# Loading weights for a split-fp32 decoder kernel: from a fixed lead of four half products to a lead set by free buffers

## The chip, the cores and the metric

The kernel runs on one core of a Trainium2 chip. It has a matrix engine (PE, with its weight loads shown apart as PEld), a vector engine (DVE), a scalar engine (ACT), GpSimd (POOL), and SyncE (SP), which here only issues DMAs. The metric is the device time of one execution in microseconds (us). Where time is broken down, it is one execution recorded by the hardware profiler.

## The reference

Two decoder layers on 512 tokens of width 2048, in fp32. Each layer projects its input to three groups of heads, attends, gates, projects back and normalizes (cut to what is computed):

```python
def hybrid_layer(x, mem, w_in, b_forget, w_mem_kv, w_out, ln_gain, ln_bias):
    h = jnp.einsum('bsd,dn->bsn', x, w_in)
    (fq, fk, fv, fg, f_logit, dq, dk, dv, dg,
     iq, ik, iw, mq, mg) = jnp.split(h, offsets, axis=-1)
    log_f = jax.nn.log_sigmoid(f_logit + b_forget)
    y_fox = fox_attention(fq, fk, fv, jnp.cumsum(log_f, axis=1)) * jax.nn.silu(fg)
    y_dsa = dsa_attention(rope(dq), rope(dk), dv, rope(iq), rope(ik), iw * 16 ** -0.5) * jax.nn.silu(dg)
    k_mem, v_mem = jnp.split(jnp.einsum('bmd,dn->bmn', mem, w_mem_kv), 2, axis=-1)
    y_mem = memory_attention(mq, k_mem, v_mem) * jax.nn.silu(mg)
    y = jnp.einsum('bsn,nd->bsd', jnp.concatenate([y_fox, y_dsa, y_mem], -1), w_out)
    return layer_norm(ALPHA * x + y, ln_gain, ln_bias)

def reference(x, mem, w_in, ...):
    for l in range(2):
        x = hybrid_layer(x, mem, w_in[l], ...)
    return x
```

The fox heads have a causal bias from the cumulated forget gates, the dsa heads choose 128 keys per query by an index score, and the memory heads attend to 256 fixed tokens.

## The kernel before

**Products of split numbers.** Each fp32 operand is split in a high and a low part, and a product is high x high, high x low and low x high. The weights come in 274 chunks of 128 x 2048 (1 MB), each used as two half products of 128 x 1024 (512 KB), so there are 548; half product n is half n % 2 of chunk n // 2. Most take 12 matmuls, those of the indexer 24. The value, gate and output projections run as seven products on 2 x 2 blocks in place of eight, so their operands are sums of blocks.

**Where a half product's weights come from.** Four ways, listed per chunk by `stream()`: 146 chunks are read from the weights as they are ("wall"); 44 from a sum that POOL's DMAs had added up in DRAM earlier ("sum", L553 to L571); 20 are loaded raw, with two further tiles ("other", L379) that DVE adds (`pair_w`, "pair"); and 64 are a raw buffer that is kept and has another block added to it ("grown", in `grow_w` by a DMA that accumulates, in `make_w` by DVE), which needs no load.

**The way of a load.** `load_w` takes one of seven raw buffers and issues the load on SP (L373). ACT copies it to a high part (`whi`), DVE subtracts that from the raw data to get the low part (`wlo`); both go to a pool of four pairs (`split_w`, helper at L242). A buffer is free once its low part is written, or, where it is to grow, once the grown product is split. In the main loop (L1602), half product n first has the loads for chunk i + 2 issued, that is for half product n + 4; for a "pair" and for the first chunks, both halves go out at the first one (L1640 to L1645). Then come the split of n + 3, the additions for a pair of n + 4, the matmuls of n, and a choice of other work.

**What sets the order.** A planner with a clock for PE, ACT, DVE and POOL (class `Clock`, L197) fits the other work between the products; it charges nothing for SP. SP works through a single list in the order in which the program was written out, and an entry whose target is not free, or whose source is not yet written, holds all behind it. Besides the raw loads, this list has the transposed reads of stored values (`load_turned`, L1378), the decay rows of the fox heads (ck, L935), head tiles (L1349, L1389), stored partial sums (L1323), and, for the normalization that runs on into layer 1, the gain and bias rows (L1455) and the residual tiles z (L1519).

**Stages.** Layer 0: values and gates from about 160 to 530 us, heads (the last value products with attention between them) to 810, output projection to 930. Layer 1: memory, indexer and small projections to 1060, values to 1471, heads to 1751, output to 1884.

Of the kernel before, what the change touches and what calls it, by code (L numbers as in the profile page):

```python
# [35 lines left out]
SCALE = HD ** -0.5  # L36
SOON, LATER, URGENT, DUE = 1.5, 4.0, 5.0, 10.0
SLOTS = 69
PACE = 2
R_ATTEND, R_QK, R_LOAD, R_MEM = 4, 5, 4, 8  # L40

# [216 lines left out]
def kernel(  # L258
# [13 lines left out]
    clock = Clock()  # L272
    nc = Engines(tc.nc, clock)
    consts = ctx.enter_context(tc.tile_pool(name="consts", bufs=1))
    raws = ctx.enter_context(tc.tile_pool(name="raws", bufs=7))
    whl = ctx.enter_context(tc.tile_pool(name="whl", bufs=4))
    slots = ctx.enter_context(tc.tile_pool(name="slots", bufs=SLOTS))
    tiny = ctx.enter_context(tc.tile_pool(name="tiny", bufs=3))
# [52 lines left out]
    chunks = stream()  # L331
    raw, parts = {}, {}
# [22 lines left out]
    def load_w(i, pieces=2, some=(0, 1)):  # L355
        if i < len(chunks) and chunks[i][4][0] != "grown":
            kind, key = chunks[i][4]
            src = {"wall": lambda: wall[key], "sum": lambda: sums[key],
                   "pair": lambda: wall[key[0]]}[kind]()
            if chunks[i][0] == "out" and chunks[i][2][0] == "P7":  # L360
                for h in some:
                    t = [slot("grown") for _ in range(2)]
                    raw.setdefault(i, []).append(t)
                    for c in range(2):
                        nc.sync.dma_start(t[c], half(src, h)[:, c * 512:(c + 1) * 512])
                return
            w = DM // pieces
            for c in range(pieces):
                if c * 2 // pieces not in some:
                    continue  # L370
                if c * 2 % pieces == 0:
                    raw.setdefault(i, []).append(raws.tile([P, H], F32, tag="raw", name=uid("raw")))
                nc.sync.dma_start(raw[i][-1][:, c * w % H:c * w % H + w], src[:, c * w:(c + 1) * w])  # L373
                if i < 3 and c * 2 % pieces == 0:
                    load_mem(2 * i + c * 2 // pieces)
                if kind == "pair":
                    for e in (2 * c, 2 * c + 1):
                        t = others[i, e] = slot("other")
                        nc.sync.dma_start(t, wall[key[1]][:, e * 512:(e + 1) * 512])  # L379

    others = {}

    def pair_w(n):

        i, h = divmod(n, 2)
        if i < len(chunks) and chunks[i][4][0] == "pair":
            for e in range(2):
                d = raw[i][h][:, e * 512:(e + 1) * 512]
                nc.vector.tensor_tensor(d, d, others.pop((i, 2 * h + e)), op=ALU.add)
# [163 lines left out]
    def add_weights(key, src):  # L553
        nc.gpsimd.dma_start(sums[key], src, accum_op=ALU.add, max_dma_last_dim=2 * DM)

    def weight_sums(kind, l, names, pairs, some=(0, 1)):

        for name in names:
            for n in some:
                step = SUM_STEPS[name][n]  # L560
                for pair in pairs:
                    for g in range(2):
                        key = (kind, l, name, pair, g)
                        src = block(kind, l, pair, g, step)
                        pool_waits()
                        if n:
                            add_weights(key, src)
                        else:
                            sums[key] = dram.tile([P, DM], F32, name=uid("sum"))
                            nc.gpsimd.dma_start(sums[key], src, max_dma_last_dim=2 * DM)  # L570
                        yield  # L571
# [1030 lines left out]
    for i, (kind, l, j, col, _) in enumerate(chunks):  # L1602
        late = last_half(i)
        if kind == "out":
            step = OUT_ORDER.index(j)
            name, pair = j
# [28 lines left out]
        for h in range(2):  # L1635
            n = 2 * i + h
            grow_w(n + 2)
            if n in late_makes:
                make_w(late_makes[n])
            if i > 0:  # L1640
                late_half = i > 8 and i + 2 < len(chunks) and chunks[i + 2][4][0] != "pair"
                if late_half:
                    load_w(i + 2, 2, (h,))
                elif h == 0:
                    load_w(i + 2)  # L1645
            if h == 0 and i > 0:
                if 2 <= i < 6:
                    for k in range(4 * i - 8, 4 * i - 4):
                        load_xt(k)
                elif i == 7:  # L1650
                    load_tables()
            if n < 6:
                split_mem(n + 2)
            if n in splits:
                finish_flow(splits.pop(n))
            if ahead_of(i):
                splits[n + 3] = flow(split_steps(n + 3), 1e9, clock.at["PE"] + DUE)
            else:
                split_w(n + 3)
            pair_w(n + 4)  # L1660
            for k in range(2 * n - 20, 2 * n - 18) if n < 16 else range(12, 16) if n == 16 else ():
                if k >= 0:
                    split_x(k)
            if kind == "out" and late:

                for e, w in enumerate(parts[n]):
                    kept.append((left[aname, 2 * col + h], e, w))
                    rows_product(zs[0], 0, kept[-1:], len(kept) == 1, h == col == e == 1, not opens)
                if h == col == 1:
                    residual(0, (2, 3)[name == "Q3"], zs[0], last=True)  # L1670
                if len(kept) == 16:
                    finish_at_once(0)
                    rows_product(chains["b", 1][1], 1, kept[:8], True, True)
                    residual(1, 2, chains["b", 1][1], last=True)
                    for c in (0, 256):
                        ps = bank("z")
                        c = slice(c, c + 256)
                        rows_product(ps, 1, kept[8:], True, True, c=c)
                        residual(1, 3, ps[:, c], 1, c, True)
                    finish_at_once(1)  # L1680
            elif kind == "out":
                for st in range(2):
                    for e in range(2):
                        r = slice(e * 256 + st * P, e * 256 + (st + 1) * P)
                        product(zs[st], tuple(a[:, r] for a in left[aname, 2 * col + h]),
                                tuple(a[:, e * 512:(e + 1) * 512] for a in parts[n]),
                                opens and col == h == e == 0,
                                col == h == e == 1, not opens)
                        advance()
            elif kind == "vs":  # L1690
                for st in range(2):
                    for e in range(2):
                        product(zs[st], val_left(aname, 2 * col + h, e, st),
                                tuple(a[:, e * 512:(e + 1) * 512] for a in parts[n]),
                                opens and col == h == e == 0, col == h == e == 1, not opens)
                        advance()
                    if col == h == 1:
                        val_out(name, pair, st, zs[st])
            elif kind == "mv":
                for m in range(2):  # L1700
                    for nn in range(2):
                        k = 4 * col + 2 * h + nn
                        c = (k % 2) * 256 + m * P
                        product(out_ps[m], tuple(a[:, c:c + P] for a in memT[k // 2]),
                                tuple(a[:, nn * 512:(nn + 1) * 512] for a in parts[n]),
                                k == 0, k == KT - 1)
            elif kind == "mk":
                for kk in range(8):
                    k = 8 * h + kk
                    m = memT[k // 2]  # L1710
                    c = (k % 2) * 256
                    product(ps[:, :256], weight_cols(n, kk), tuple(a[:, c:c + 256] for a in m),
                            k == 0, k == KT - 1)
            else:
                cols = slice(P if kind == "iq" else 0, SEQ)
                for kk in range(8):
                    k = 8 * h + kk
                    product(ps[:, cols], weight_cols(n, kk), tuple(a[:, cols] for a in xT[k]),
                            k == 0, k == KT - 1)
                    advance()  # L1720
            del parts[n]
            if h == 0:
                tick(kind, kind in ("out", "vs"))
# [174 lines left out]
```

## Time and profile before

| what | value |
|---|---|
| median of 3 runs | 1885.79 us (1884.57 to 1889.16) |
| the profiled execution: own time, span | 1885.75 us, 1884.0 us |
| mean granted clock of PE | 0.997 |
| ACT, whi from raw | 497 times, 1056 ns each |
| DVE, wlo from raw and whi | 497 times, 1217 ns each |
| PE, one matmul of the value products, 128 x 512 | about 227 ns from start to start |
| raw loads on SP, 512 KB each | 331 from the weights, 72 from sums |
| issue to landing of a raw load, median | 7.3 and 7.4 us |
| loads of "other", 256 KB each | 80, 13.7 us to landing |
| data moved | 478.40 MB, mean 254 GB/s |

A matmul's start-to-start time comes from 12 matmuls in 2.72 us. A row of a wait names who waits (engine, tile, line), then behind the arrow whose work ended the wait, and the total, the number and the longest. In a timeline, the numbers in brackets are the idle time ahead of an instruction and what ended it. "SPq" is SyncE's DMA issue. Names such as raw, whi, wlo, z, ck are the program's tile names. Nearly all compute instructions carry the line of one helper, L242, so they are told apart by their tiles.

### The profile page before, as it was taken

The numbers are of one execution on the slowest core, as the hardware profiler recorded it, in microseconds if no ns is written. First come the engines' busy times: TensorE is split into PE (matmuls) and PEld (weight loads), VectorE is DVE, ScalarE is ACT, GpSimd is POOL, SyncE is SP. The second block draws the span as 40 slices with busy tenths as digits, with TensorE's granted clock in tenths as the row PEclk, the third lists the DMA queues.
The fourth block names the chain that finished last, engine by engine and source line by source line (L and its number), as shares of the span: only waits on it lengthen the run. The fifth ranks groups of instructions, "written<-read, shape, count | busy, mean of one in ns | idle before, by whom it ended". The sixth has DMA issues, their size and how long they took to land.

```text
span 1884.0 us, 26451 instructions
## 1 busy us (share of the span) xinstructions
PE 1854.5 (98%) x8994; PEld 1574.5 (84%) x8994; DVE 1606.9 (85%) x2565; ACT 1079.0 (57%) x1752; POOL 404.9 (21%) x595
## 2 busy tenths in 40 slices
PE   9999999999999999999999999999999999999997
PEld 8998888887888888888899977877878888888886
DVE  6789889888789987889887997898797898878798
ACT  5776344435347887555476653444354578875553
POOL 0121222122134311330011121221221343113302
PEclk9999999999999999999999999999999999999999
DMA  9885998898999978986598869988989998889866
GB/s 350 294 240 160 302 298 242 303 279 274 253 239 298 241 217 218 268 209 214 174 322 250 228 204 302 329 270 288 284 274 246 247 306 226 222 213 276 237 215 144
DMA packets 232165, 478.40 MB, mean 254 GB/s; under 512 B 76624, under 2 KB 101200, under 8 KB 231772
## 3 DMA queue, kind: packets, MB, share of 16 engines
q1 hardware_dynamic: 177660, 302.58, 49.8%
q0 software_dynamic: 53792, 173.06, 35.7%
q8 instruction: 71, 1.16, 0.2%
q10 hardware_dynamic: 576, 1.05, 0.1%
q14 instruction: 66, 0.54, 0.1%
HBM read 404.24 MB, written 152.07 MB: 295 GB/s over the span
## 4 chain that ended last, share of the span: by engine, by line
PE 70%; DVE 14%; DMA 8%; issue 4%; ACT 3%; SPq 0%; POOL 0%; DVEq 0%; ACTq 0%; POOLq 0%
PE v L242 30%; PE c L242 17%; PE z L242 15%; DVE wlo L242 6%; DMA other<-in_wall_dram 4%; DMA raw<-in_wall_dram 3%; PE po L242 3%; DVE raw L242 2%; PE s L242 2%; DVE acc L242 1%; ACT whi L242 1%; PE ix L242 1%; PE pt L242 1%; DMA v<-vraw 1%; DVE rope L242 1%
## 5 line engine op out<-in xcount | busy, mean ns | idle before, releaser
L242 ACT ACTIVATE whi<-raw 128x1024 fp32r<-128x1024 f32 (+1 forms) x497 | 521.2, 1056 | 473.5 <-PE v L242 190.9
L242 DVE TENSOR_TENSOR wlo<-raw,whi 128x1024 fp32r<-128x1024 f32 (+1 forms) x497 | 601.0, 1217 | 115.8 <-ACT whi L242 113.6
L242 PE MATMUL v<-whi,vxh 128*128 128x512 f32 x768 | 306.3, 399 | 6.8 <-ACT whi L242 3.2
L242 PE MATMUL v<-wlo,vxh 128*128 128x512 f32 x768 | 301.4, 392 | 7.9 <-DVE wlo L242 7.9
L242 PE MATMUL v<-whi,vxl 128*128 128x512 f32 x768 | 300.5, 391 | 0.0
L242 PE MATMUL v<-whi,xh 128*128 128x512 f32 x576 | 224.2, 389 | 0.0
L242 PE MATMUL v<-whi,xl 128*128 128x512 f32 x576 | 224.1, 389 | 0.0
L242 PE MATMUL v<-wlo,xh 128*128 128x512 f32 x576 | 224.1, 389 | 0.0
L242 PE MATMUL c<-xh,whi 128*128 128x512 f32 (+1 forms) x544 | 197.9, 364 | 0.0
L242 PE MATMUL c<-xh,wlo 128*128 128x512 f32 (+1 forms) x544 | 197.8, 364 | 0.0
L242 PE MATMUL c<-xl,whi 128*128 128x512 f32 (+1 forms) x544 | 197.7, 363 | 0.0
L242 POOL TENSOR_TENSOR seen<-mark,mhalf 128x1 f32<-128x1 f32 x88 | 48.3, 549 | 636.3 <-ACT mark L242 447.3
L242 PEld LDWEIGHTS v<-whi,vxh 128*128 128x128 f32 x768 | 144.7, 188 | 40.1 <-ACT whi L242 7.2
L242 PEld LDWEIGHTS v<-wlo,vxh 128*128 128x128 f32 x768 | 144.9, 189 | 39.3 <-DVE wlo L242 12.5
L242 PE MATMUL z<-wlo,yh 128*128 128x512 f32 (+1 forms) x434 | 167.8, 387 | 2.3 <-DVE wlo L242 2.3
L242 PEld LDWEIGHTS v<-whi,vxl 128*128 128x128 f32 x768 | 144.5, 188 | 30.4
L242 PE MATMUL z<-whi,yh 128*128 128x512 f32 (+1 forms) x434 | 168.6, 389 | 0.0
L242 PE MATMUL z<-whi,yl 128*128 128x512 f32 (+1 forms) x434 | 167.7, 387 | 0.0
L242 PEld LDWEIGHTS v<-wlo,xh 128*128 128x128 f32 x576 | 108.1, 188 | 22.6
L242 PEld LDWEIGHTS v<-whi,xh 128*128 128x128 f32 x576 | 108.1, 188 | 22.5
L242 PEld LDWEIGHTS v<-whi,xl 128*128 128x128 f32 x576 | 108.1, 188 | 22.5
L242 PEld LDWEIGHTS c<-xl,whi 128*128 128x128 f32 x544 | 102.1, 188 | 12.2
(209 smaller groups left out, 3459.9 us busy)
## 6 DMA issues: line engine op xcount, KB each, us to landing
raw<-in_wall_dram SPq DMA_DIRECT2D x331, 512.0 KB, 7.3
sum<-in_wall_dram POOLq DMA_DIRECT2D x88, 1024.0 KB, 10.4
raw<-sum SPq DMA_DIRECT2D x72, 512.0 KB, 7.4
v<-vraw POOLq DMA_DIRECT2D x88, 256.0 KB, 8.8
other<-in_wall_dram SPq DMA_DIRECT2D x80, 256.0 KB, 13.7
vt<-halves POOLq DMA_DIRECT2D x56, 256.0 KB, 9.4
vraw<-v SPq DMA_DIRECT2D x56, 256.0 KB, 5.1
grown<-in_wall_dram POOLq DMA_DIRECT2D x48, 256.0 KB, 8.9
```

The source lines that it names most:

```text
L242: return f(*args, **kw)
```

## The change

A half product's load is issued by a new function `load_half`, which remembers in `loaded` what is out. The load for n + 4 stays. After it, when chunk 8 is past, `load_more` looks ahead from n + 4 and issues up to two further half products, up to n + 14, skipping those that grow. It stops where fewer than two of the seven raw buffers would be left by the program's count (`raws_used() >= RAWS - 1`), at one product of the output projection, at a pair while more than two of the "other" tiles are outstanding, and at a sum whose last addition the planner issued less than 20 us ago by its own clock (`settled`). A pair's two halves now also go out one by one.

```diff
+RAWS, FAR, SETTLE = 7, 14, 20.0
...
-    raws = ctx.enter_context(tc.tile_pool(name="raws", bufs=7))
+    raws = ctx.enter_context(tc.tile_pool(name="raws", bufs=RAWS))
...
+    loaded, settled = set(range(6)), {}
+
+    def load_half(m):
+        if m not in loaded:
+            loaded.add(m)
+            load_w(m // 2, 2, (m % 2,))
+
+    def raws_used():
+        return len({id(t) for v in raw.values() for t in v if t is not None and not isinstance(t, list)})
+
+    def load_more(n):
+
+        m = n + 4
+        for _ in range(2):
+            while m in loaded or (m < 2 * len(chunks) and chunks[m // 2][4][0] == "grown"):
+                m += 1
+            if m > n + FAR or m >= 2 * len(chunks) or raws_used() >= RAWS - 1:
+                return
+            kind, l, j, _, (how, key) = chunks[m // 2]
+            if kind == "out" and j[0] == "P7" or how == "pair" and len(others) > 2:
+                return
+            if how == "sum" and settled.get(key, 1e9) + SETTLE > clock.at["PE"]:
+                return
+            load_half(m)
...
                             add_weights(key, src)
+                            settled[key] = clock.at["PE"]
...
             if i > 0:
-                late_half = i > 8 and i + 2 < len(chunks) and chunks[i + 2][4][0] != "pair"
-                if late_half:
-                    load_w(i + 2, 2, (h,))
-                elif h == 0:
-                    load_w(i + 2)
+                for m in (n + 4,) if i > 8 else (n + 4, n + 5) if h == 0 else ():
+                    load_half(m)
...
             pair_w(n + 4)
+            if i > 8:
+                load_more(n)
```

Lines below move by one (L373 is L374) and further down by 27 (L1378 is L1405, L935 is L962, L1455 is L1482, L1519 is L1546). The instructions of PE, ACT, DVE and POOL stand in the same order as before; the list of SP has the same 753 rows in another order. Three places of it follow. A row has the line, the operation, the target and its source, and the shape; numbers at the names count tiles in the order of writing.

SP where layer 0's heads begin (raw: weights, from the weights or a sum; vraw: values of a head read transposed; ck: decay rows), before:

```order
L373 DMA raw_5107<-sum_1132 128x1024
L1378 DMA_TRANSPOSE vraw_5116<-vt_168 128x1x1024
L1378 DMA_TRANSPOSE vraw_5118<-vt_170 128x1x1024
L935 DMA ck_5120<-crow_159 128x512
L1378 DMA_TRANSPOSE vraw_5122<-vt_168 128x1x1024
L1378 DMA_TRANSPOSE vraw_5124<-vt_170 128x1x1024
L935 DMA ck_5126<-crow_159 128x512
L373 DMA raw_5157<-sum_1132 128x1024
L373 DMA raw_5244<-sum_1264 128x1024
L373 DMA raw_5281<-sum_1264 128x1024
```

and with the change:

```order
L374 DMA raw_5002<-sum_1142 128x1024
L374 DMA raw_5028<-sum_1142 128x1024
L374 DMA raw_5052<-sum_1274 128x1024
L374 DMA raw_5074<-sum_1274 128x1024
L374 DMA raw_5096<-in_wall_dram 128x1024
L374 DMA raw_5121<-in_wall_dram 128x1024
L1405 DMA_TRANSPOSE vraw_5126<-vt_168 128x1x1024
L1405 DMA_TRANSPOSE vraw_5128<-vt_170 128x1x1024
L962 DMA ck_5130<-crow_159 128x512
L1405 DMA_TRANSPOSE vraw_5132<-vt_168 128x1x1024
L1405 DMA_TRANSPOSE vraw_5134<-vt_170 128x1x1024
L962 DMA ck_5136<-crow_159 128x512
```

The second half of the first sum, both halves of the next sum and two loads of plain weights now stand ahead of the four transposes and of both decay rows: five loads that stood behind them.

SP in layer 1 ahead of the first value products (row: gain and bias of layer 0's normalization; z: a tile of its residual), before:

```order
L1519 DMA z_10760<-x_183 128x512
L373 DMA raw_10786<-in_wall_dram 128x1024
L373 DMA raw_10851<-sum_9319 128x1024
L373 DMA raw_10910<-sum_9319 128x1024
L1455 DMA row_10952<-in_gain_dram 128x512
L1455 DMA row_10954<-in_bias_dram 128x512
L1519 DMA z_10956<-x_183 128x512
L373 DMA raw_10978<-in_wall_dram 128x1024
L373 DMA raw_11003<-in_wall_dram 128x1024
L373 DMA raw_11046<-sum_10096 128x1024
L373 DMA raw_11068<-sum_10096 128x1024
```

and with the change:

```order
L1546 DMA z_10522<-x_183 128x512
L374 DMA raw_10553<-sum_9329 128x1024
L374 DMA raw_10611<-sum_9329 128x1024
L374 DMA raw_10678<-in_wall_dram 128x1024
L374 DMA raw_10742<-in_wall_dram 128x1024
L1546 DMA z_10770<-x_183 128x512
L374 DMA raw_10921<-sum_10106 128x1024
L1482 DMA row_10958<-in_gain_dram 128x512
L1482 DMA row_10960<-in_bias_dram 128x512
L1546 DMA z_10962<-x_183 128x512
L374 DMA raw_10989<-sum_10106 128x1024
```

Of the four raw loads that stood behind the rows, the two of plain weights and the first half of the sum now stand ahead of them; the sum's second half stays behind.

SP in layer 1's values, the stretch that was issued around 1180 to 1199 us, before:

```order
L1455 DMA row_11985<-in_gain_dram 128x512
L1455 DMA row_11987<-in_bias_dram 128x512
L1519 DMA z_11989<-x_183 128x512
L373 DMA raw_11994<-in_wall_dram 128x1024
L373 DMA raw_12014<-in_wall_dram 128x1024
L373 DMA raw_12042<-in_wall_dram 128x1024
L373 DMA raw_12060<-in_wall_dram 128x1024
L373 DMA raw_12084<-in_wall_dram 128x1024
L379 DMA other_12086<-in_wall_dram 128x512
L379 DMA other_12088<-in_wall_dram 128x512
```

and with the change:

```order
L1546 DMA z_11853<-x_183 128x512
L374 DMA raw_11879<-in_wall_dram 128x1024
L374 DMA raw_11902<-in_wall_dram 128x1024
L374 DMA raw_11920<-in_wall_dram 128x1024
L374 DMA raw_11953<-in_wall_dram 128x1024
L374 DMA raw_11975<-in_wall_dram 128x1024
L380 DMA other_11977<-in_wall_dram 128x512
L380 DMA other_11979<-in_wall_dram 128x512
L1482 DMA row_11999<-in_gain_dram 128x512
L1482 DMA row_12001<-in_bias_dram 128x512
L1546 DMA z_12003<-x_183 128x512
```

The rows and the z tile, which stood ahead of five raw loads and the other tiles of a pair, now stand behind them.

## The prediction

> **What bounds the kernel now.** I read the page first (the span, part 1), then the busy times by stretch, then the waits of the stretches where the matrix engine sits idle. Each stretch row has its length, the busy time of PE, PEld, DVE, ACT and POOL with counts, the granted clock, the DMA share and GB/s.
>
> ```profile
> span 1884.0 us, 26451 instructions
> PE 1854.5 (98%) x8994; PEld 1574.5 (84%) x8994; DVE 1606.9 (85%) x2565; ACT 1079.0 (57%) x1752; POOL 404.9 (21%) x595
> ...
> 530.00:810.00 280.00, 278.03 (x1415) 235.04 (x1414) 240.03 (x442) 204.01 (x397) 73.44 (x98) 1.00 0.91 251
> 1060.00:1090.00 30.00, 30.00 (x154) 26.96 (x153) 27.60 (x44) 19.47 (x36) 4.26 (x7) 1.00 0.90 261
> 1090.00:1115.00 25.00, 22.65 (x102) 18.21 (x101) 24.12 (x36) 13.67 (x24) 6.02 (x9) 1.00 0.56 178
> 1165.00:1190.00 25.00, 23.47 (x95) 19.03 (x96) 23.91 (x33) 13.21 (x18) 5.81 (x10) 0.93 0.88 220
> 1190.00:1236.00 46.00, 44.59 (x196) 36.30 (x194) 36.23 (x55) 18.60 (x22) 10.86 (x16) 1.00 1.02 341
> 1236.00:1380.00 144.00, 140.21 (x611) 114.31 (x612) 125.68 (x172) 65.69 (x84) 28.52 (x49) 1.00 0.86 270
> 1751.00:1884.00 133.00, 120.23 (x553) 99.70 (x551) 116.55 (x195) 58.34 (x87) 31.88 (x42) 0.97 0.71 189
> ```
>
> PE is busy 1854.5 of 1884.0 us, so nothing that only shortens its waits can bring more than 29.5 us, and 12.77 of those (133.00 less 120.23) are the tail of the output product and of the normalization, of which the new loads touch nothing. The change only moves weight loads on SP. It can pay where a load is late for its split (ACT writes whi from raw, DVE then wlo from both), and that split is late for PE. The waits of 1060 to 1240 (total, times, longest):
>
> ```profile
> ACT whi L242 <- DMA raw<-in_wall_dram: 10.9, 8, 3.4
> DVE raw L242 <- DMA other<-in_wall_dram: 9.8, 7, 2.2
> ...
> PE v L242 <- DVE wlo L242: 3.9, 4, 1.8
> PE v L242 <- ACT whi L242: 1.6, 2, 0.8
> ```
>
> Of 10.9 + 9.8 us that ACT and DVE wait for weights here, PE feels 3.9 + 1.6 = 5.5 us. This is where loads bind. In the heads of layer 0 (530 to 810; layer 1's heads are the same code) PE's idle time is 280.00 - 278.03 = 1.97 us, and its releasers are results that go out of PSUM, no splits:
>
> ```profile
> PE v L242 <- ACT vraw L242: 0.8, 2, 0.5
> PE v L242 <- DVE vraw L242: 0.6, 1, 0.6
> PE v L242 <- DVE rec L242: 0.5, 1, 0.5
> ```
>
> **The change part by part.** The profiled execution took 1885.75 us (span 1884.0 and 1.75 around it); the sum is made against that. The median of the runs shown, 1885.79, is 0.04 us away. The orders of PE, ACT, DVE and POOL are unaltered, and SP issues the same DMAs, so no instruction is added or removed on any engine: only times of landing move. SP stands here with its idle time and work:
>
> ```profile
> 1047.46 1.07 SPq L373 DMA_DIRECT2D raw<-in_wall_dram  x1
> 1048.63 0.85 SPq L373 DMA_DIRECT2D raw<-sum  x2
> 1065.61 0.33 SPq L1455 DMA_DIRECT2D row<-in_gain_dram  x1
> ...
> 1067.53 1.24 SPq L373 DMA_DIRECT2D raw<-in_wall_dram  x2
> 1068.86 5.17 SPq L373 DMA_DIRECT2D raw<-sum  x2
> ...
> SPq L1455 <- DVE rope L242: 16.1, 1, 16.1
> SPq L1519 <- DMA x<-z: 7.3, 1, 7.3
> ```
>
> Term a, start of layer 1's values. SP stood 16.1 us at the load of a gain row, whose slot the rotary work freed late. Four weight loads stood behind it and went out at 1067.5 to about 1074. In the second order shown with the change, three of the four stand ahead of that row; they need only buffers, which splits free, and go out 11 to 19 us earlier. Their lateness shows as ACT's idle time in brackets, then in DVE, then in PE:
>
> ```profile
> 1080.88 1.06 ACT L242 ACTIVATE whi<-raw 128x1024 fp32r<-128x1024 f32 x1 [3.36 <-DMA raw<-in_wall_dram]
> 1084.72 2.24 ACT L242 ACTIVATE whi<-raw 128x1024 fp32r<-128x1024 f32 x2 [1.55 <-DMA raw<-in_wall_dram]
> ...
> 1085.82 1.23 DVE L242 TENSOR_TENSOR wlo<-raw,whi 128x1024 fp32r<-128x1024 f32 x1 [0.48 <-ACT whi L242]
> ...
> 1108.43 0.50 PE L242 MATMUL v<-wlo,vxh 128*128 128x512 f32 x1 [0.59 <-DVE wlo L242]
> 1113.21 0.50 PE L242 MATMUL v<-wlo,vxh 128*128 128x512 f32 x1 [1.76 <-DVE wlo L242]
> ```
>
> ACT's 3.36 + 1.55 us go, but DVE, which PE waits for, is busy 24.12 of 25 us, and only 0.48 us of its idle time came from a late whi. DVE cannot catch up more than that, in the order that it keeps. I take 0.5 us; the bounds are 0 and PE's whole idle time, 2.35 us (25.00 - 22.65).
>
> Term b, 1165 to 1190: PE is idle 25.00 - 23.47 = 1.53 us, and 1.35 more are lost to the clock (term c). In the third order shown, five raw loads and the two further blocks of a pair now stand ahead of two rows and a residual load that waited. The splits that PE waits for here stand behind pairs' additions; the 9.8 us of DVE's waits for "other" tiles are the row. The first of these pairs was issued before the place where the order differs, so only part can shift: I take 0.5, bounds 0 and 1.53.
>
> Term c, the clock. After two short waits the granted clock fell in 3 us to 0.55, which costs 3.00 x (1 - 0.55) = 1.35 us:
>
> ```profile
> 1167.00:1170.00 3.00, 2.96 (x8) 2.32 (x9) 2.95 (x5) 3.00 (x6) 1.99 (x3) 0.55 0.21 70
> ...
> 1165.78 0.50 PE L242 MATMUL v<-whi,vxh 128*128 128x512 f32 x1 [0.78 <-ACT whi L242]
> 1167.04 0.59 PE L242 MATMUL v<-wlo,vxh 128*128 128x512 f32 x1 [0.76 <-DVE wlo L242]
> ...
> 1234.88 0.50 PE L242 MATMUL v<-whi,vxh 128*128 128x512 f32 x1 [0.80 <-ACT whi L242]
> 1236.14 0.50 PE L242 MATMUL v<-wlo,vxh 128*128 128x512 f32 x1 [0.76 <-DVE wlo L242]
> ```
>
> A like pair of waits at 1234.88 and 1236.14 was followed by no loss (clock 1.00 in 1236 to 1380). So the loss hangs on the moment as well as on the waits. It may go, stay, or come at the other pair too (-1.35): I take half, 0.7 us. The Trainium skill, "TensorE: Matmul & The Clock Gate", section "HAM oscillation — how this bites in real kernels", has the clock fall when the engine idles for longer than about 3.4 us; by that rule neither pair of waits could have cost a clock, term c would be 0, and the sum 1884.1. This trace differs: 0.78 and 0.76 us of idle time stand right before the fall.
>
> Term d, 1190 to 1236: PE is idle 46.00 - 44.59 = 1.41 us. Four raw loads go out 2.4 us and more earlier, one split's pace each. But the transfers run at a share of 1.02 with 341 GB/s here, against 0.56 at 178 GB/s in 1090 to 1115: what is issued early shares its engines with what was issued before. I take half, 0.7 us; bounds 0 and 1.41. The Trainium skill, "DMA: Bandwidth & Descriptors", section "Issuing engines are not separate DMA queues", says that transfers interleave on the same 16 DMA engines whoever issued them; taken strictly, a stretch at a share of 1.02 gains nothing from issuing early, d is 0 and the sum 1884.1. The row of 1.02 speaks for it, that of 0.56 leaves room one stretch earlier.
>
> Term e, the heads: 0, since no split is among PE's releasers there. The cover is loads that land before their splits, and it is not gone as raws go out earlier still. What becomes late instead is the subject of the slower rival. Term f, 1236 to 1380: PE is idle 3.79 us, but from about 1240 on the two orders agree again: 0.
>
> Sum: 0.5 + 0.5 + 0.7 + 0.7 = 2.4 us; 1885.75 - 2.4 = 1883.4.
>
> **The rivals.** First: **nothing moves**. Seven buffers hold the data of 4 loads ahead, 2 being split and little else; the new rule reaches two further at most. Where the buffers bind, a load that stands earlier in the order starts when it did before, and ACT's 10.9 us of waits for raws mostly stay. For it: PE feels only 5.5 us; DVE, at 24.12 of 25, cannot use earlier data. Against it: SP's 16.1 us at a row load, with three free weight loads behind it. Time: 1885.75, with the loads' terms all 0. Chance 0.24.
>
> Second: **all waits for weights vanish**. From 1060 to 1236, PE's idle time is 2.35 + 1.53 + 1.41, and the clock's 1.35 goes with it: 6.6 us, so 1879.1; with half of the 3.79 us after it, 1877.2. For it: each wait in that region ends at a split or at what feeds one. Against it: DVE's 0.48, and pairs' other tiles, which come no earlier than the raws that they follow. Chance 0.22.
>
> Third, on the other side: **small loads queue behind weights** where the heads begin. One queue issues in order. In the first order shown, five further raw loads stand ahead of the turned values and of the decay rows (ck). Buffers come free at the splits' pace there:
>
> ```profile
> L242 ACT ACTIVATE whi<-raw x6: 1047/1059/1064, 531.0 to 542.9; 128x1024 fp32r<-128x1024 f32 x6
> ...
> 531.97 5.84 SPq L1378 DMA_TRANSPOSE vraw<-vt  x2
> ...
> DMA to landing us min/median/max: 4.5/5.5/8.4
> ...
> 543.31 0.37 POOL L242 TENSOR_SCALAR bt<-ck,cq 128x128 f32<-128x128 f32 x1 [8.39 <-DMA ck<-crow]
> 549.08 1.14 ACT L242 ACTIVATE qh<-vraw 128x512 fp32r<-128x512 f32 x2
> ...
> 553.55 1.06 ACT L242 ACTIVATE whi<-raw 128x1024 fp32r<-128x1024 f32 x1 [3.34 <-issue]
> ...
> 563.93 0.69 DVE L242 CUSTOM_DVE_ANT_0 bt<-s,bt 128x512 f32<-128x512 f32 x1 [0.51 <-PE s L242]
> ```
>
> Six splits in 531.0 to 542.9 are 2.4 us apart, (542.9 - 531.0) / 5, so five loads hold the first transpose from 531.97 to at most 531.97 + 11.9 = 543.9. With 4.5 to 8.4 us to land, its data comes at 548.4 to 552.3, and ACT reads them at 549.08: late by 3.2 at most, and a second group behind it alike, some 2.6. Two groups, 5.8 us, in two layers are 11.6: 1897.4 where all of it reaches PE, 1891.6 where half does. It decides from the point at which a transpose is issued after 549.08 - 5.5 = 543.6, or where the decay rows, waited for until 543.31, come more than some 10 us late, since their tables feed DVE at 563.93. Against it: the 3.34 us for which ACT is idle before 553.55 swallow the first lateness, and a buffer or two may be free earlier than 2.4 us per load. Chance 0.16, and my reason for the upper end.
>
> **How the numbers follow.** The forecast has 0.38, the rivals 0.24, 0.22 and 0.16. A measurement of this kernel can tell 0.3% from no change, 5.7 us: faster is below 1880.1, slower above 1891.4. The forecast and the first rival lie within; the second lies beyond only with nearly all its waits gone (most of its 0.22), and the third mostly beyond, with what other small load might come late. This gives 0.22 faster, 0.63 the same, 0.15 slower. The likeliest case alone, with its bounds (2.35 + 1.53 + 1.35 + 1.41 gained, or 1.35 lost to the clock), spans 1879.1 to 1887.1. The range for 8 in 10 goes from the second rival's 1877.2 to the third's half price: 1877 to 1892; left out are the third's full price and combinations.
>
> **What would show it.** Term a: SP's wait of 16.1 us may stay, but three weight loads stand ahead of it, ACT's waits for raws fall from 10.9 to under 6, and PE's 2.35 us in 1090 to 1115 fall by little. Terms b and d: PE's idle time in the two later stretches shrinks by a third to a half. Term c: a clock of 1.00 where 0.55 stood. Term e: PE's idle time in the heads stays near 2 us. The third rival would show as ACT's qh in the heads waiting for the DMA into vraw, POOL's 8.39 us for ck growing toward 20, and PE idle in 545 to 610. The forecast is wrong if DVE makes use of earlier data beyond 0.48 us, or if a transfer that nobody was late for before (rows, residuals, turned values) becomes late for an engine that works in order.

## The result and the profile after

The change made the kernel slower: 1900.7 us median of 6 runs against 1886.16 for the kernel before, ratio 1.0069 with a 95% interval of 1.0052 to 1.0086. The forecast was 1883.4 us in a range of 1877 to 1892; it was wrong. One of the six runs took 6083.61 us; the ratio goes by the other five, and nothing on record shows what held that run up. A later set of runs of the same kernel (f1 below) gave 1.0051 (1.0035 to 1.0068).

The head of the changed kernel's page:

```profile
span 1899.7 us, 26470 instructions
PE 1862.2 (98%) x8994; PEld 1579.9 (83%) x8994; DVE 1607.9 (85%) x2565; ACT 1082.4 (57%) x1752; POOL 398.7 (21%) x595
```

PE is busy 7.7 us longer for the same matmuls, and idle for the other half of the 15.7 us. Its busy times by stretch (length, busy PE, PEld, DVE, ACT, POOL, granted clock, DMA share, GB/s; the work of a stretch lies up to 13 us later than before, so a row does not hold quite the same work):

```profile
530.00:810.00 280.00, 274.17 (x1383) 231.32 (x1382) 236.79 (x439) 199.69 (x386) 71.04 (x102) 0.99 0.91 244
1090.00:1115.00 25.00, 25.00 (x116) 20.90 (x115) 24.63 (x38) 14.73 (x25) 2.25 (x4) 1.00 0.56 153
1165.00:1190.00 25.00, 24.16 (x106) 19.43 (x105) 21.49 (x29) 11.23 (x15) 3.69 (x6) 1.00 0.81 214
1190.00:1236.00 46.00, 44.47 (x188) 36.08 (x187) 36.40 (x58) 18.47 (x22) 11.67 (x19) 0.96 1.03 350
1236.00:1380.00 144.00, 140.58 (x604) 114.68 (x603) 121.25 (x165) 60.87 (x75) 28.45 (x45) 0.98 0.87 268
```

The stretch of the heads, where PE had lost 1.97 us, now loses 280.00 - 274.17 = 5.83, and its clock is 0.99. In the two stretches at 1090 and 1165 the idle time went from 2.35 to 0 and from 1.53 to 0.84 (in part because the waits moved out of them: PE is 8 us late by then), and the clock of 0.93 is 1.00.

Since PE's order is unaltered in every kernel here, each matmul can be paired with the same one of before, and the lag of its start read off. This table has by how much the lag grew in each stretch (times of the trace of before), in us: for the change, for its second execution f1, and as the mean, with the lowest and highest, over all traces of this study with further loads in that stretch and over those without (the experiments follow below):

| stretch | change | f1 | with further loads there | without |
|---|---|---|---|---|
| 428 to 445, layer 0's values | +3.0 | 0.0 | +3.0 (0.0 to 5.1), 6 traces | +1.1 (-0.2 to 3.9), 7 |
| 535 to 815, layer 0's heads | +5.5 | +4.7 | +5.5 (4.7 to 6.1), 4 | +0.3 (-0.4 to 0.9), 6 |
| 1100 to 1166, layer 1's values | -1.3 | -1.4 | -1.4 (-1.8 to -1.1), 7 | 0.0 (-0.9 to 1.1), 6 |
| 1166 to 1175 | -1.6 | -1.6 | -1.6 | -1.6 (all 13 within 0.1) |
| 1219 to 1250, rows and residual tiles | +7.6 | +4.5 | +5.7 (4.5 to 7.6), 4 | +1.1 (0.0 to 2.8), 9 |
| 1250 to 1465 | -1.7 | +0.4 | -1.6 (-3.1 to 0.4), after such a loss, 4 | 0.0 (-2.9 to 4.5), 9 |
| 1465 to 1745, layer 1's heads | +5.3 | +3.3 | +4.3 (3.3 to 5.3), 4 | +0.8 (0.2 to 1.5), 6 |
| the rest | -1.0 | -0.1 | | |
| sum | +15.8 | +9.8 | | |

In the rows of the heads, e1, e6 and e7 are left out, which have a part of the further loads there. The row at 1166 is alike in all: the profiled execution of before had a fall of the clock there that no other has, so its 1.6 us are luck and no gain of the change.

In the heads the waits name the mechanism. SP's timeline of the changed kernel, where before the first two transposes had gone out at 531.97:

```profile
534.46 6.57 SPq L374 DMA_DIRECT2D raw<-sum  x4
543.43 2.30 SPq L374 DMA_DIRECT2D raw<-in_wall_dram  x2
545.78 4.87 SPq L1405 DMA_TRANSPOSE vraw<-vt  x2
550.75 0.53 SPq L962 DMA_DIRECT2D ck<-crow  x1
```

Of the view of the tile vraw, 545 to 562 us, the row on its transfers:

```profile
DMA to landing us min/median/max: 4.1/5.6/6.0
```

The transposes go out 13.8 us later, 10.9 of them beyond the lag of 2.9 that PE had by then. They land as fast as before (median 5.6 us against 5.5): the lateness is all from standing behind raw loads on SP. Who waited is in the timelines of POOL, ACT, DVE and PE from there on and, last, of PE in layer 1's heads (idle time ahead and its releaser in brackets):

```profile
554.70 0.37 POOL L243 TENSOR_SCALAR bt<-ck,cq 128x128 f32<-128x128 f32 x1 [16.92 <-DMA ck<-crow]
...
555.51 0.63 ACT L243 ACTIVATE qh<-vraw 128x512 fp32r<-128x512 f32 x1 [2.95 <-DMA vraw<-vt]
...
578.75 0.63 ACT L243 ACTIVATE tanh<-vraw 128x512 f32<-128x512 f32 x1 [1.03 <-DMA vraw<-vt]
580.38 0.63 ACT L243 ACTIVATE vh<-vraw 128x512 fp32r<-128x512 f32 x1 [0.99 <-DMA vraw<-v]
...
585.95 0.50 PE L243 MATMUL v<-whi,vxh 128*128 128x512 f32 x1 [1.68 <-ACT vraw L243]
...
610.78 0.63 ACT L243 ACTIVATE qh<-vraw 128x512 fp32r<-128x512 f32 x1 [2.48 <-DMA vraw<-vt]
...
614.80 0.63 ACT L243 ACTIVATE vh<-vraw 128x512 fp32r<-128x512 f32 x1 [1.39 <-DMA vraw<-v]
...
617.34 1.23 DVE L243 TENSOR_TENSOR wlo<-raw,whi 128x1024 fp32r<-128x1024 f32 x1 [2.61 <-ACT whi L243]
...
619.83 0.50 PE L243 MATMUL v<-whi,vxh 128*128 128x512 f32 x1 [2.61 <-DVE vraw L243]
...
1568.59 0.50 PE L243 MATMUL v<-whi,vxh 128*128 128x512 f32 x1 [3.21 <-DVE vraw L243]
```

ACT's waits of 540 to 625 us (total, times, longest):

```profile
ACT qh L243 <- DMA vraw<-vt: 5.4, 2, 3.0
ACT vh L243 <- DMA vraw<-v: 2.4, 2, 1.4
ACT tanh L243 <- DMA vraw<-vt: 1.3, 2, 1.0
```

Before, ACT waits for none of these tiles in that stretch. Now ACT, which works in order, waits for a turned tile or a head tile six times, its weight splits and evictions slip behind, DVE waits for a split (at 617.34), and PE stands. After 619.83 the clock falls too: the lag grows by another 1.5 us with PE busy.

### The profile page after: what moved, and what is told of

It is laid out like the page before. It is cut to its first block, busy times and chain, and to the rows that moved or that the text cites. A ratio compares the mean times of both kernels' runs of the same rounds, so it can differ in the third digit from the quotient of the medians.

```text
span 1899.7 us, 26470 instructions
## 1 busy us (share of the span) xinstructions
PE 1862.2 (98%) x8994; PEld 1579.9 (83%) x8994; DVE 1607.9 (85%) x2565; ACT 1082.4 (57%) x1752; POOL 398.7 (21%) x595
## 5 line engine op out<-in xcount | busy, mean ns | idle before, releaser
L243 PE MATMUL v<-whi,vxh 128*128 128x512 f32 x768 | 309.0, 402 | 15.8 <-DVE vraw L243 5.8
```

Of the source, the lines that this page charges most:

```text
L243: return f(*args, **kw)
```

## The experiments

"Theory Q" is that of the third rival: small loads which other engines need in order stand behind raw loads on SP. "Theory C" is contention: more 512 KB transfers in flight make everything land later, anywhere. Each run is told as a ratio to runs of the kernel before on the same chip. In all of them the orders of PE, ACT, DVE and POOL are those of before.

**e1: the change without the heads' products.**

```diff
+            if kind == "vs" and j[0] in ("Q5", "Q3"):
+                return
```

> The full change, but no further load is issued when its target is one of the heads' products (Q5, Q3); the order of SP in the heads is as before the change. Theory Q (small loads that other engines need in order stand behind raw loads on SP): of the 15.7 us that the trace of the change lost, matmul by matmul 5.9 came in layer 0's heads and 4.9 in layer 1's, so this run should be 10.8 us faster than the change, about 1889 to 1891, and PE's idle time in the heads back near 2 us each. Theory C (the loss is contention and lost clock spread over the kernel): the run stays near 1897 to 1900.

1.0030 (1.0016 to 1.0044), 1893.91 us, against 1.0069 and 1.0051 for the whole change. The heads' waits for transposes are gone, but the run did not get down to 1889. PE's waits show a new one:

```profile
PE gt L243 <- DMA vraw<-v: 4.8, 2, 2.5
```

At the end of each layer's heads, three further raw loads for the output projection now stand ahead of two head tiles which PE itself turns: theory Q at a place that I had not listed. The expectation missed by this. The wait is e1's own: at these two matmuls PE waits 2.26 and 2.50 us in e1, and not at all in either trace of the whole change.

**e2: further loads around the heads alone.** The rule by which a pair's halves go out is that of before here, and in e3, e6, e7, f2, f3 and f4.

```diff
-            if i > 8:
+            if 157 <= n <= 217 or 431 <= n <= 491:
                 load_more(n)
```

> Further loads only while the products just ahead of the heads and those of the heads run (both layers), all else as before the change. Theory Q: plus 10.8 us over before, about 1896 to 1897, with ACT waiting some 3 us for a transposed value tile at the heads' start and POOL's wait for the decay rows near 17 us instead of 8.4. Theory C: a part in proportion to the further loads here, some 57 of about 230 per layer pair, so plus 3 to 5 us, and no wait for transposes.

1.0050 (1.0032 to 1.0068), 9.4 us by the ratio. The heads alone give most of what the change lost, and the waits are those that theory Q expected; theory C expected none for transposes:

```profile
ACT qh L243 <- DMA vraw<-vt: 4.6, 2, 2.8
ACT vh L243 <- DMA vraw<-v: 3.8, 2, 3.0
...
POOL bt L243 <- DMA ck<-crow: 31.9, 3, 16.8
```

**e3 and f4: only the start of layer 1.** The same kernel on two chips.

```diff
-            if i > 8:
+            if 283 <= n <= 340:
                 load_more(n)
```

> Further loads only from layer 1's first products to its 11th or so half product after the indexer, half products 283 to 340; later stretches, the heads and layer 0 as before. Theory Q: here loads overtake rows that nobody is late for, so PE gains what the change gained between 1100 and 1170 us, 3.1 us (0.8 of a wait, 0.75 of another, 1.5 of the clock): about 1883. Theory C: no gain, 1886 or above.

> The same kernel as e3, once more on another chip. Theory Q: the gain of e3 repeats, 0.997 to 0.999. If e3 was luck of its runs, 1.000.

0.9983 (0.9969 to 0.9998), then 0.9993 (0.9980 to 1.0006). From 1100 to 1166 us both profiled executions win at the expected place, 1.8 and 1.5 us, where the six traces without these loads have 0.0 on the mean. The 1.5 us of clock in the expectation were none of the change's (the row at 1166 us of the table). By the traces the gain is some 1.4 us (the mean of seven in the row from 1100 to 1166), by the two ratios 3.2 and 1.3; the second interval includes none, and that this kernel beats the one before is likely and not settled.

**e4: only the pairs' halves one by one.**

```diff
-            if i > 8:
-                load_more(n)
```

> Only the smallest part of the change: a pair's two halves are issued one by one, no further loads at all. Theory Q: SP's order differs in two rows, so no difference, 1885 to 1887. A rival: the second half of a pair comes one half product later and DVE's waits for the other tiles, 33.1 us before, grow, so slower by some us.

0.9996 (0.9985 to 1.0008): no difference.

**e5 and f2: the normalization's rows.** e5 leaves out half products 336 to 372 from the change; f2 keeps only these, with `if 336 <= n <= 372`.

```diff
-            if i > 8:
+            if i > 8 and not 336 <= n <= 372:
                 load_more(n)
```

> The full change, but no further loads for half products 336 to 372, so that the gain and bias rows and the residual tiles of layer 0's normalization keep their place ahead of the raw loads around 1150 to 1240 us. Theory Q: DVE's wait of 8.1 us for the residual tile at 1214 to 1222 us goes, and with it the two waits of PE and falls of the clock behind it that cost the change 7.2 us between 1220 and 1250; so 5 to 7 us faster than the change (about 1.000 + 0.0069 - 0.003 = 1.004 of before). Rival (bandwidth: these waits come from a share of 1.03 in that stretch): DVE waits there as long, and the time stays at 1.006 to 1.007.

> Further loads only for half products 336 to 372, where two rows and a residual tile of the normalization come to stand behind raw loads; all else as before. Theory Q: DVE waits some 8 us for the residual tile near 1215 us and PE loses 2 to 6 us there, of which 1 to 2 come back at later waits: 1.001 to 1.003. If e5 is taken at its word (leaving these loads out saved nothing), 1.000.

e5: 1.0066 (1.0046 to 1.0086), no gain against the change, though in its trace DVE's wait for the residual tile is gone, as expected. f2: 1.0002 (0.9990 to 1.0015). The mechanism is there: DVE, in order, waits for the residual tile that was overtaken. First the changed kernel, then f2:

```profile
1221.79 1.42 DVE L243 TENSOR_TENSOR z<-z,row 128x512 f32<-128x512 f32 x2 [8.13 <-DMA z<-x]
```

```profile
DVE z L243 <- DMA z<-x: 8.8, 1, 8.8
```

But it costs next to nothing in the end. In f2's trace PE loses 5.6 us between 1219 and 1250 us, and 3.1 of these come back up to 1465 us, as waits that were there before (at 1303 and 1358 us) vanish for work that comes later anyway. On the mean of the table it is 5.7 - 1.1 lost and 1.6 won back, 3 us; the measured interval of f2 leaves 2.8 us at most. The 7.6 us in the trace of the change overstate this place.

**e6: the heads with n + 6 in place of n + 14.** As e2, and:

```diff
-RAWS, FAR, SETTLE = 7, 14, 20.0
+RAWS, FAR, SETTLE = 7, 6, 20.0
```

> As e2 (further loads in the heads alone), but at most two half products further than before, n + 6 instead of n + 14. Two raw loads instead of five stand ahead of the first transposes, 2 x 2.4 = 4.8 us in place of 11.9. In the change the turned tile came 2.95 us late at a shift of 13.8 - 2.9 = 10.9 us, so it had 8 us to spare. Theory Q: the first group is late no more, and the loss falls from 9.4 us (e2) to some 0 to 4 us, what is left in the later groups. If each raw load ahead costs its share (no spare time), two fifths of 9.4 stay: 3.8 us; then ACT still waits for the first transposed tile.

1.0005 (0.9990 to 1.0019). Not two fifths of the loss (3.8 us) are left, but about none, at most 3.6 us by the interval; in the table's two rows of the heads e6 has -0.1 and +0.1. So the loss does not go in proportion to the loads ahead. SP, POOL and ACT in e6:

```profile
535.28 4.83 SPq L374 DMA_DIRECT2D raw<-sum  x3
540.16 4.77 SPq L1405 DMA_TRANSPOSE vraw<-vt  x2
...
549.02 1.86 POOL L243 TENSOR_SCALAR bt<-ck,cq 128x128 f32<-128x128 f32 x1 [10.41 <-DMA ck<-crow]
...
552.77 1.14 ACT L243 ACTIVATE qh<-vraw 128x512 fp32r<-128x512 f32 x2
```

The first transposes go out at 540.16, 8.2 us later than before (3.7 of them the lag of PE in this execution, nearly all from 430 us), and ACT reads the tile without a wait: a shift of 4.5 us is within the spare time that the expectation worked out as 8. In the whole stretch from 540 to 625 us ACT waits for no DMA.

**e7: the heads, without the first group.**

```diff
-            if i > 8:
+            if 172 <= n <= 217 or 446 <= n <= 491:
                 load_more(n)
```

> As e2, but the further loads begin only with the first product of the heads (half products 172 to 217 and 446 to 491), so that the first transposes and decay rows keep their place. Theory Q with a cost at each place: the wait of 1.9 us at 580 us goes, that at 612 us (2.9 us and 1.2 of clock) stays, likewise in layer 1: 4 to 7 us over before in place of 9.4. If the first group's lateness is the cause of all that follows, the loss goes altogether, 0 to 1 us.

1.0035 (1.0017 to 1.0053), 6.6 us. In its trace PE's wait at 580 us is gone, and that at 612 us costs 3.7 us and 1.5 more of clock. In the table's two rows of the heads e7 has +4.9 and +3.9, e2 +5.7 and +3.8. So the groups cost each for itself, and by these traces the later ones make most of the loss.

**e8: the change without the three pieces that were found.**

```diff
+            if kind == "vs" and j[0] in ("Q5", "Q3") or kind == "out" and chunks[n // 2][0] == "vs":
+                return
...
-            if i > 8:
+            if i > 8 and not 336 <= n <= 372:
                 load_more(n)
```

> The full change without three pieces: no further load for the heads' products, none for the output projection while the heads run (in e1 its three raw loads stood ahead of stored sums and PE waited 2.5 us for one at the end of each layer's heads), none for half products 336 to 372. Theory Q: all places that lose are named, only the gain at the start of layer 1's values is left, 0.998 of before as in e3, 3 us faster. If something else in the change loses (values of layer 0, memory stage), the time is 1.000 or above.

0.9996 (0.9983 to 1.0008). What loses is thereby named: against e1 (1.0030), only the output's loads during the heads and the rows are left out, and the wait of e1 is gone. The output's loads were not run alone. The expected 0.998 lies just outside the interval, a gain of 1.4 us, as in the traces of e3 and f4, within it.

**f1: the change again, with no edit; f3: layer 0's products only.** For f3:

```diff
-            if i > 8:
+            if i > 8 and n <= 156:
                 load_more(n)
```

> The change as it is, on the same chip as the three below, so that parts and whole have one base. 1.006 to 1.007 of before; ACT in the heads waits for turned tiles again, DVE waits some 8 us for a residual tile near 1220 us.

> Further loads only up to half product 156, in layer 0's indexer and value products; SP's order differs in a single row. In the traces of the change, of e1, e5 and e8 a raw load went out at 415.1 to 416.0 us instead of 418.9 and PE waited 1.3 to 2.9 us at 430 us; but e6, which has the order of before there, did the same. If the further loads cause it: the early issue and the wait show again, 1.001 to 1.003. If it is chance: 1.000 and no wait beyond 0.7 us.

f1: 1.0051 (1.0035 to 1.0068), a little less than expected, with the same waits of ACT for turned tiles and 6.1 us of DVE's for the residual tile. f3: 0.9998 (0.9985 to 1.0011), no loss, though its trace does show the early raw load and a wait of 2.0 us at 430 us. f1, which has the whole change, shows no such wait (0.46 us). Over all 14 traces the long wait (1.2 us and more) is in 5 of the 6 kernels with further loads in layer 0's values and in 3 of the 8 without. So it comes under both orders; what brings it, and whether the change makes it more frequent, stays open.

## Why the prediction was wrong

**Term e, the heads at 0, is the step that failed.** It looked at who released PE before the change, and found no splits, so it saw nothing to win; that part holds. But the change also moved the small loads of the heads behind raw loads, and their cost was left to a rival with 0.16. Measured, the heads cost 9.4 us alone (e2) where the sum had nothing, and that is most of the loss: 1.0050, against 1.0069 and 1.0051 for the whole change.

**The third rival was right in place and mechanism, and in size by two errors that cancel.** It had the transposes at up to 543.9 us: they went out at 545.78, with PE 2.9 us late. It had ACT late by up to 3.2 us at its first read and by 2.6 in a second group: 2.95 and 2.48 were measured. It had POOL's wait for ck growing toward 20 us: 16.92.

Yet these are not what cost the time. The idle time that I held against the rival swallowed the first, and another, which I had not looked at, nearly all of the second, as ACT's lag shows: 5.9 us at 555.51 and back to 2.9 at the next split (whose 3.34 us of idle time are 0.28 now); from 5.2 to 7.8 at 610.78 and back to 5.7 at the next instruction (2.06 us before, none now). What cost were the tiles right behind these, at 578.75, 580.38 and 614.80 to 615.73: 1.03 + 0.99 and 1.39 + 0.30 us of waits at places where ACT had no idle time left (before, it had none from 564.7 to 581.7 us). They raised its lag from 3.4 to 5.7 and from 5.7 to 7.6, PE waited 1.68 and 2.61 us for what ACT and DVE hand it (0.61 of the second were there before), and 1.5 us of clock came on top. The later of the two waits is in every trace with all the further loads of the heads; of the earlier one f1 has only 0.09 us. So the full price, 11.6 us in two layers, stands near the 9.4 of e2 (10.8 and 8.0 in the two traces of the change), but it is made of later tiles and of the clock; that the sizes agree is luck. I had looked at the first tile of each group, found room for it, and priced the case as improbable.

**Terms a and b were right, c was luck.** From 1100 to 1166 us the change wins 1.4 us on the mean of seven traces, against 1.0 forecast. In the trace of the change PE's wait of 0.59 us at 1108 is 0.02, that of 0.78 us at 1166 is 0.07. Term a was bounded by DVE as argued: ACT's 3.36 us of idle time are 0.03 and DVE's 0.48 are gone, and the wait of 1.76 us at 1113 us is still there. ACT's waits for raw loads fell less than forecast, from 10.9 us to 8.4 (1068 to 1253 us, the same work) and not to under 6. The second rival, that all these waits vanish, did not come: 1.76 us at 1113 and 0.76 us at 1167 stay. The clock's fall at 1167 us (0.7 of the forecast) is in none of the 13 other traces, those with the order of before included; it was a chance of that one execution.

**Term d had the wrong sign.** I looked at the raw loads that come earlier (0.7 us), not at the residual tile that they overtake. Its lateness appeared only in the last sentence of the prediction, without a price. The price is some 4.6 us on the spot, of which at most 2.8 stay (f2).

**Term f** (no difference from 1250 us to the heads) holds within the spread of the traces, but for what comes back there. At 430 us the prediction expected nothing; what the traces show there comes under both orders, and f3 measured no loss.

**The first rival** (buffers bind, nothing moves) was half right, and that half is why the loss arose. It said that the new rule reaches two loads further at most; two is the limit per half product, and five stand ahead of the transposes, as the third rival counted. The further loads did wait for buffers, which are free once `wlo` is written. SP's waits of 528 to 546 us (total, times, longest), before and with the change:

```profile
SPq L373 <- DVE wlo L242: 5.0, 1, 5.0
```

```profile
SPq L374 <- DVE wlo L243: 13.4, 5, 5.0
```

But a load that waits at the head of SP's list holds all that stands behind it: the four loads at 534.46 and the two at 543.43 took until 545.73, over 11 us.

## What to carry to other kernels

A queue that issues in order makes each early load a barrier as long as it waits for its buffer: count what is queued behind it, and compare the delay with the spare time of every small load there, group by group. A buffer that counts as free because the instruction that frees it stands earlier in the program may not be free when the issue comes up. The wait for it is not yet a loss: in the heads a lead of n + 6 cost nothing that could be measured, and one of n + 14 cost 9 us, though loads waited for buffers with both. Idle time of the reader that absorbs the first late tile says nothing of what the next one costs.

## What was not expected of the hardware

The clock of PE fell here after two short waits, none longer than 2.92 us. At 430 us all 14 traces have the same two waits of PE, 1.3 us apart, the first of different length. The stretch of 427 to 441 us in the changed kernel, then in e1:

```profile
427.00:441.00 14.00, 11.34 (x42) 8.69 (x41) 12.30 (x17) 8.14 (x12) 1.20 (x3) 0.88 0.56 189
```

```profile
427.00:441.00 14.00, 11.90 (x52) 9.31 (x51) 12.86 (x18) 8.84 (x13) 2.10 (x4) 1.00 0.59 202
```

| the two waits, us | traces | granted clock, 427 to 441 us |
|---|---|---|
| 0.34 to 0.65, and about 0.80 | 6 | 1.00 |
| 1.22 and 1.29, and about 0.80 | 2 | 1.00 |
| 1.86 to 2.92, and 0.65 to 0.80 | 6 | 0.76 to 0.88 |

At this place the clock stayed up to 2.1 us of idle time in the two waits and fell from 2.7 us on. By the lag of the matmuls behind, the fall cost 1.6 us beyond the waits where the clock was 0.88 and 2.8 us where it was 0.76. The Trainium skill, "TensorE: Matmul & The Clock Gate", section "HAM oscillation — how this bites in real kernels", puts the bound at a single idle gap of about 3.4 us; no gap here is that long, and the measurement decides. It is not a fixed sum of idle time either: at 1167 us of the kernel before, the clock fell after 0.78 and 0.76 us, and at the same place e4, e6 and f3 waited 0.90 and 0.75 to 0.76 us and kept a clock of 1.00. What else decides stays open. By the trace of the change, 0.007 of its span of 1899.7 us was lost to the clock, 13 us, against 0.003 of 1884.0, 6 us, before: about half of the difference of that pair of executions. In f1 it is 0.004 of 1893.7, 8 us, a fifth of its difference.
